# Two 256-column gate tiles in the halves of one PSUM bank instead of in two banks

## The chip, the cores and the metric

The kernel runs on one core of a Trainium2 chip. The metric is the device time of one execution in microseconds (us): the median of the runs, lower is better. A second execution of each kernel is recorded by the hardware profiler; the rows below come from it.

The engines in this text are PE (TensorE, the matrix unit; it writes its results only into PSUM, the accumulator memory of eight banks), ACT (ScalarE), DVE (VectorE), POOL (GpSimd) and SP (which issues the DMA transfers). Each engine works through its own list of instructions in order; a semaphore makes an instruction wait for one on another engine.

## The reference, cut to what matters

One decoder layer on 256 tokens of width 1024, all in float32: a SwiGLU feed-forward block, three parallel token mixers, and a second feed-forward block, with a layer norm after each.

```
h = x @ w_in + b_in
q_a, k_a, v_a, q_b, k_b, v_b, q_m, gates = split(h)
y_a = sliding_window_gqa(q_a, k_a, v_a, attn_sinks) @ w_proj_swa
y_b = moba_attention(q_b, k_b, v_b) @ w_proj_moba
y_m = memory_cross_attention(q_m, mem, ...) @ w_proj_mem
g = sigmoid(gates.reshape(B, S, 3, 1024))
mixed = (g[:, :, 0] * y_a + g[:, :, 1] * y_b + g[:, :, 2] * y_m) @ w_out
x = layer_norm(ALPHA * x + mixed, ln2_g, ln2_b)
```

The change is in the projection that makes `gates`: 3 branches of 1024 columns for 256 tokens.

## The kernel before

Every float32 weight or activation is held as a high part (`whi`, made by an ACT cast) and a low part (`wlo`, made by a DVE subtraction); `split` makes both. `product` computes one float32 product as three matmuls, high x high, high x low and low x high (lines L209, L210 and L211 in the profile). All weights come in one stream of chunks of 128 x 2048 values, which SP loads in order, ACT and DVE split two chunks ahead, and PE uses.

PSUM is one pool of eight banks, `mm` (also called `acc`). Every `mm.tile([P, 512], F32)` takes one bank, whether or not all 512 columns are used, and gives it back when its last reader is done.

The gates are made feature by token: a **tile** here is 128 features x 256 tokens, 8 input blocks x 3 = 24 matmuls of 256 columns. `gate_chunk(c, b, js)` makes the two tiles j = 0 and 1 of one weight chunk; c is one of four groups of 256 features, b one of three branches. The result goes through `tanh` on ACT (with the bias and a factor of a half, which makes a sigmoid up to scale) into `gates`. Groups c = 0 and 1 use `feature_tile` and the left 256 columns of a bank; groups 2 and 3 use another way of multiplying, with all 512 columns, and are not touched.

The six chunks of groups 0 and 1 are placed by hand between the steps of the three attentions, to give PE work while ACT and DVE do the softmax. `scores(nm)` multiplies queries and keys of mixer a, b or m on PE (L637) and has DVE and ACT do the softmax; `turn(nm, i)` transposes two heads' probabilities on PE (L684) and splits them into `p`; `weigh(nm, i)` multiplies `p` by the values on PE (`ps<-p,vab`) and splits the result into `qk_a` or `qk_b`. The code asks for this order:

```
    turn("a", 2)
    gate_chunk(0, 0)
    weigh("a", 2)
    scores("b")
    gate_chunk(0, 1)
    scores("m")
    gate_chunk(0, 2)
    turn("b", 0)
    gate_chunk(1, 0)
    weigh("b", 0)
    turn_b1 = turn("b", 1)
    gate_chunk(1, 1, (0,))
```

In chunks (1, 1) and (1, 2) the two tiles are asked for apart, with a `weigh` and a `turn` between them. The order on each engine (all but SP) is not the code's own: a scheduler that goes by an estimate of readiness, with the code's order as priority, writes it when the program is built, and inserts the semaphore waits. It keeps two engines from using the same bank at a time.

Of the kernel before, what the change touches and what calls it, by code (L numbers as in the profile page):

```python
# [10 lines left out]
F32 = mybir.dt.float32  # L11
F32R = mybir.dt.float32r
BF16 = mybir.dt.bfloat16
AF = mybir.ActivationFunctionType
# [3 lines left out]
P = 128  # L18
S = 256
# [101 lines left out]
def hybrid_layer(ctx: ExitStack, tc: tile.TileContext, a: dict, out: bass.AP):  # L121
    nc = tc.nc
# [9 lines left out]
    mm = acc = ctx.enter_context(tc.tile_pool(name="mm", bufs=8, space=PSUM))  # L132
# [63 lines left out]
    def weights(key, ahead=2):  # L196
        i = index[key]
        load_to(i + 6)
        part_to(i + ahead)
        return part_of.pop(i)  # L200
# [4 lines left out]
    def product(ps, terms, first=True, last=True):  # L205

        n = len(terms)
        for i, ((lh, ll), (rh, rl)) in enumerate(terms):
            nc.tensor.matmul(ps, lh, rh, start=first and i == 0, stop=False)  # L209
            nc.tensor.matmul(ps, lh, rl, start=False, stop=False)  # L210
            nc.tensor.matmul(ps, ll, rh, start=False, stop=last and i == n - 1)  # L211

    def two(t, *s):
        return tuple(x[s] for x in t)
# [6 lines left out]
    def feature_tile(ps, w, col, x, n=KD):  # L221

        product(ps, [(two(w, ALL, slice(k * 256 + col, k * 256 + col + P)), two(x, ALL, k, ALL)) for k in range(n)])

    def feature_tile_2(ps, w, col, x, ks=range(KD), parts_=(0, 1)):

        for part in parts_:
            for k in ks:
                wk = w[part][:, k * 256 + col : k * 256 + col + P]
                if part == 0:  # L230
                    nc.tensor.matmul(ps, wk, x.both[:, k], start=k == 0, stop=False)  # L231
                else:
                    nc.tensor.matmul(ps[:, S:], wk, x[0][:, k], start=False, stop=k == KD - 1)  # L233

    def added(dst, ps):

        b = work.tile([P, 512], F32, name="b", tag="w")[:, :S]
        nc.scalar.copy(b, ps[:, S:])  # L238
        nc.vector.tensor_add(dst, ps[:, :S], b)
# [23 lines left out]
    def tokens_of(name):  # L263

        both = acts.tile([P, KD, 2, S], F32R, name=name, tag="xT")
        return Parts(both)
# [39 lines left out]
    bcol = const.tile([P, NB], F32, name="bcol")  # L306
# [246 lines left out]
    x1T = tokens_of("x1T")  # L553
# [17 lines left out]
    for j in range(2):  # L571
        ps = mm.tile([P, 512], F32, name="ps")
# [4 lines left out]
    for t in range(2):  # L577
        ps = mm.tile([P, 512], F32, name="ps")
# [127 lines left out]

    gates = acts.tile([P, 2, 6, S], F32, name="gates", tag="A1")

    gate_w = {}

    def gate_chunk(c, b, js=(0, 1)):
        if js[0] == 0:
            gate_w[c, b] = weights(("gt", c, b))
        pss = [mm.tile([P, 512], F32, name="ps") for _ in js]
        if c >= 2:
            for part in range(2):
                for j, ps in zip(js, pss):
                    feature_tile_2(ps, gate_w[c, b], j * P, x1T, parts_=(part,))
        for j, ps in zip(js, pss):
            k = 12 + 8 * b + 2 * c + j  # L720
            g = gates[:, c % 2, 2 * b + j, :]
            if c < 2:
                feature_tile(ps[:, :S], gate_w[c, b], j * P, x1T)
                nc.scalar.activation(g, ps[:, :S], AF.Tanh, bias=bcol[:, k : k + 1], scale=0.5)  # L724
            else:
                added(g, ps)
                nc.scalar.activation(g, g, AF.Tanh, bias=bcol[:, k : k + 1], scale=0.5)
# [14 lines left out]
    weigh("a", 1)  # L742
# [9 lines that stand above are left out]
# [115 lines left out]
```

## Time and profile before

| | |
|---|---|
| median of 3 runs | 573.05 us (572.82 to 573.26) |
| the profiled execution's own time | 573.67 us |
| span of its profile, first to last instruction | 571.9 us |
| PE busy | 561.0 us, 98% of the span |
| DVE busy | 451.7 us, 79% |
| ACT busy | 323.6 us, 57% |
| mean granted TensorE clock | 0.996 of full speed |

The span is 1.8 us less than the execution's own time; what lies around it is start and end. Times in a row count from the span's start. A row of the timeline gives the start of an instruction, how long it lasted, engine, line, operation, tile written and tiles read, shape and number; in brackets how long the engine had stood idle before, and for whom. Instructions of an engine overlap: a matmul of 256 columns lasts 0.28 us, but the next starts 0.12 us after it.

### The profile page before, as it was taken

The page shows a single profiled execution, that of the slowest core. Times are in us where ns is not written, and L with a number is a line of the kernel's source. Part 1 is how long each engine was busy: PE and PEld are TensorE (multiplying, and loading weights), DVE is VectorE, ACT ScalarE, POOL GpSimd, SP SyncE. Part 2 cuts the span into 40 slices and gives each one's busy share as a digit, 9 for nine tenths or more (in the row PEclk, how much of TensorE's full clock was granted, in tenths as well). Part 3 has the DMA queues.
Part 4 walks back from the last instruction along what each step waited for, and adds up shares of the span by engine and source line. Part 5 has one row for each costly group of instructions (what it writes and reads, how often), then busy time and mean ns, then how long its engine had stood idle before and what let it go on. Part 6 is the DMA issues. An engine that isn't in the chain of part 4 may idle for free.

```text
span 571.9 us, 8715 instructions
## 1 busy us (share of the span) xinstructions
PE 561.0 (98%) x3378; PEld 498.4 (87%) x3378; DVE 451.7 (79%) x707; ACT 323.6 (57%) x569; POOL 23.6 (4%) x37
## 2 busy tenths in 40 slices
PE   8999999999999999999999999999999999999994
PEld 7888888888888998999999999888898888888883
DVE  4798768788888998699787677997577777889686
ACT  5777555546653652964975655553564645564600
POOL 2000000000000000000002022210000000000001
PEclk9999999999999999999999999999999999999998
DMA  7877856535665276084053655436654645444502
GB/s 266 301 279 290 291 190 252 179 122 197 223 238 221 74 273 242 6 339 172 15 230 127 220 181 189 177 155 253 234 187 175 219 157 211 148 149 170 198 0 73
DMA packets 18025, 108.98 MB, mean 191 GB/s; under 512 B 2112, under 2 KB 2368, under 8 KB 5696
## 3 DMA queue, kind: packets, MB, share of 16 engines
q1 hardware_dynamic: 17984, 108.43, 51.9%
q8 instruction: 26, 0.43, 0.3%
q14 instruction: 15, 0.12, 0.1%
HBM read 107.37 MB, written 1.05 MB: 190 GB/s over the span
## 4 chain that ended last, share of the span: by engine, by line
PE 92%; ACT 3%; DVE 2%; DMA 1%; issue 0%; SPq 0%; POOLq 0%; DVEq 0%
PE ps L231 29%; PE ps L210 15%; PE ps L209 15%; PE ps L233 15%; PE ps L211 15%; ACT whi L136 1%; DMA xT<-in_xT_dram 1%; ACT sc_b L660 1%; PE ps L684 1%; PE ps L277 1%; DVE sc_b L644 1%; DVE m L649 0%; PE ps L637 0%; ACT gates L724 0%; DVE r L519 0%
## 5 line engine op out<-in xcount | busy, mean ns | idle before, releaser
L136 ACT CAST whi<-raw 128x512 fp32r<-128x512 f32 (+3 forms) x242 | 193.8, 845 | 144.3 <-PE ps L231 73.3
L137 DVE TENSOR_TENSOR wlo<-raw,whi 128x512 fp32r<-128x512 f32 (+3 forms) x242 | 230.1, 984 | 54.3 <-ACT whi L136 51.5
L231 PE MATMUL ps<-x0T,whi 128*128 128x512 f32 x352 | 85.8, 392 | 1.6 <-DVE x0T L137 0.8
L231 PEld LDWEIGHTS ps<-x0T,whi 128*128 128x128 f32 x352 | 64.1, 188 | 14.1 <-ACT whi L136 2.1
L231 PE MATMUL ps<-x2T,whi 128*128 128x512 f32 x288 | 68.8, 391 | 0.0
L231 PEld LDWEIGHTS ps<-x2T,whi 128*128 128x128 f32 x288 | 53.0, 188 | 10.3
L209 PE MATMUL ps<-x1T,whi 128*128 128x256 f32 x192 | 55.2, 288 | 0.3 <-ACT sc_m L660 0.3
L211 PE MATMUL ps<-x1T,wlo 128*128 128x256 f32 x192 | 54.4, 283 | 0.0
L210 PE MATMUL ps<-x1T,whi 128*128 128x256 f32 x192 | 54.4, 283 | 0.0
L210 PE MATMUL ps<-wlo,hh 128*128 128x512 f32 (+1 forms) x142 | 54.1, 381 | 0.0
L209 PE MATMUL ps<-whi,hh 128*128 128x512 f32 (+1 forms) x142 | 54.0, 381 | 0.0
L211 PE MATMUL ps<-whi,hl 128*128 128x512 f32 (+1 forms) x142 | 54.0, 380 | 0.0
L233 PEld LDWEIGHTS ps<-x0T,wlo 128*128 128x128 f32 x352 | 46.1, 191 | 2.6 <-DVE wlo L137 0.3
L233 PE MATMUL ps<-x0T,wlo 128*128 128x256 f32 x352 | 46.9, 283 | 0.0
L233 PEld LDWEIGHTS ps<-x2T,wlo 128*128 128x128 f32 x288 | 36.9, 191 | 1.4
L209 PEld LDWEIGHTS ps<-x1T,whi 128*128 128x128 f32 x192 | 36.8, 192 | 0.8 <-ACT sc_m L660 0.5
L233 PE MATMUL ps<-x2T,wlo 128*128 128x256 f32 x288 | 37.4, 283 | 0.0
L210 PEld LDWEIGHTS ps<-x1T,whi 128*128 128x128 f32 x192 | 36.8, 192 | 0.0
L211 PEld LDWEIGHTS ps<-x1T,wlo 128*128 128x128 f32 x192 | 36.8, 192 | 0.0
L238 ACT COPY b<-ps 128x256 f32<-128x256 f32 x92 | 30.7, 368 | 1.0 <-PE ps L233 0.6
L211 PEld LDWEIGHTS ps<-whi,hl 128*128 128x128 f32 x142 | 26.7, 188 | 5.1
L209 PEld LDWEIGHTS ps<-whi,hh 128*128 128x128 f32 x142 | 26.7, 188 | 5.1
(195 smaller groups left out, 888.1 us busy)
## 6 DMA issues: line engine op xcount, KB each, us to landing
raw<-in_w_dram SPq DMA_DIRECT2D x92, 1024.0 KB, 4.8
raw<-in_w_dram SPq DMA_DIRECT2D x16, 256.0 KB, 5.3
ln<-in_ln_dram SPq DMA_DIRECT2D x3, 1024.0 KB, 6.9
xT<-in_xT_dram SPq DMA_DIRECT2D x4, 256.0 KB, 7.1
x_sb<-in_x_dram SPq DMA_DIRECT2D x1, 1024.0 KB, 7.0
mem<-in_memT_dram SPq DMA_DIRECT2D x1, 1024.0 KB, 6.9
out_dram<-r SPq DMA_DIRECT2D x3, 256.0 KB, 2.1
brow<-in_by_column_dram SPq DMA_DIRECT2D x1, 387.0 KB, 7.7
```

Of the source, the lines that this page charges most:

```text
L136: nc.scalar.copy(hi, src)
L137: return nc.vector.tensor_sub(lo, src, hi.bitcast(F32))
L209: nc.tensor.matmul(ps, lh, rh, start=first and i == 0, stop=False)
L210: nc.tensor.matmul(ps, lh, rl, start=False, stop=False)
L211: nc.tensor.matmul(ps, ll, rh, start=False, stop=last and i == n - 1)
L231: nc.tensor.matmul(ps, wk, x.both[:, k], start=k == 0, stop=False)
L233: nc.tensor.matmul(ps[:, S:], wk, x[0][:, k], start=False, stop=k == KD - 1)
L238: nc.scalar.copy(b, ps[:, S:])
L277: nc.tensor.transpose(ps[:, j * P : (j + 1) * P], src[:, k * P : (k + 1) * P], ident)
L644: nc.vector.scalar_tensor_tensor(sc[:, len(raw), :], dist[nm], -SLOPES[h] / SCALE, ps[:, :w], op0=ALU.mult, op1=ALU.add)
L660: nc.scalar.activation(sc[:, e, c0:c1], raw[e][:, c0:c1], AF.Exp, bias=negm[:, e, t : t + 1], scale=SCALE, accum_out=ssum[:, e, t : t + 1])
L684: nc.tensor.transpose(pt[:, s * n + j * P : s * n + (j + 1) * P], sc[:, 2 * i + s, c : c + P], ident)
```

## The change

For groups c = 0 and 1 both tiles of a chunk share one bank: tile 0 takes columns 0 to 255, tile 1 columns 256 to 511. The bank is taken when tile 0 is asked for and kept in `gate_ps`. The number and size of the matmuls, the activations, splits and transfers stay as they are. Lines after L709 move down by five (L724 becomes L729).

```diff
-    gate_w = {}
+    gate_w, gate_ps = {}, {}
 
     def gate_chunk(c, b, js=(0, 1)):
         if js[0] == 0:
             gate_w[c, b] = weights(("gt", c, b))
-        pss = [mm.tile([P, 512], F32, name="ps") for _ in js]
-        if c >= 2:
+        if c < 2:
+
+            if js[0] == 0:
+                gate_ps[c, b] = mm.tile([P, 512], F32, name="ps")
+            pss = [gate_ps[c, b][:, j * S : (j + 1) * S] for j in js]
+        else:
+            pss = [mm.tile([P, 512], F32, name="ps") for _ in js]
             for part in range(2):
...
             if c < 2:
-                feature_tile(ps[:, :S], gate_w[c, b], j * P, x1T)
-                nc.scalar.activation(g, ps[:, :S], AF.Tanh, bias=bcol[:, k : k + 1], scale=0.5)
+                feature_tile(ps, gate_w[c, b], j * P, x1T)
+                nc.scalar.activation(g, ps, AF.Tanh, bias=bcol[:, k : k + 1], scale=0.5)
```

The scheduler puts other work between the two tiles of a chunk. In the listings below a number behind a name tells tiles apart, and the bracket names the engines whose semaphores the instruction waits for.

On PE around chunk (0, 0) of before, where `ps_2669` and `ps_2670` are its two tiles and `ps_2721` is `weigh("a", 2)`:

```order
L211 MATMUL ps_2669<-x1T_1837,wlo_2474 128x256
L209 MATMUL ps_2670<-x1T_1837,whi_2473 128x256
...
L211 MATMUL ps_2670<-x1T_1837,wlo_2474 128x256
L209 MATMUL ps_2721<-p_2646,vab_2008 128x512 [waits Activation_49]
L210 MATMUL ps_2721<-p_2647,vab_2008 128x512 [waits DVE_49]
L211 MATMUL ps_2721<-p_2646,vab_2008 128x512
L209 MATMUL ps_2721<-p_2653,vab_2008 128x2x128 [waits Activation_49]
```

The same place on PE with the change, where `ps_2669` is the bank of both tiles and `ps_2720` is `weigh("a", 2)`:

```order
L211 MATMUL ps_2669<-x1T_1837,wlo_2474 128x256
L209 MATMUL ps_2720<-p_2646,vab_2008 128x512 [waits Activation_49]
L210 MATMUL ps_2720<-p_2647,vab_2008 128x512 [waits DVE_49]
L211 MATMUL ps_2720<-p_2646,vab_2008 128x512
L209 MATMUL ps_2669<-x1T_1837,whi_2473 128x256 [waits Activation_49]
...
L209 MATMUL ps_2720<-p_2653,vab_2008 128x2x128
```

Three of the six matmuls of `weigh("a", 2)` now stand between the tiles, and the first matmul of tile 1 waits for ACT. Around chunk (0, 1) it is the same with five of the 24 matmuls of `scores("m")` between the tiles.

On PE around `turn("b", 0)` of before, where `ps_2945` is tile 1 of chunk (0, 2), `sc_b` the softmax of mixer b, and `ps_3024` tile 0 of chunk (1, 0):

```order
L211 MATMUL ps_2945<-x1T_1837,wlo_2660 128x256
L684 MATMUL ps_2996<-ident_95,sc_b_2732 128x128 [waits DVE_49,Activation_49]
L684 MATMUL ps_2996<-ident_95,sc_b_2732 128x128 [waits DVE_49] x3
L684 MATMUL ps_3005<-ident_95,sc_b_2732 128x128 [waits Activation_49]
L684 MATMUL ps_3005<-ident_95,sc_b_2732 128x128
L209 MATMUL ps_3024<-x1T_1837,whi_2815 128x256 [waits Activation_49]
```

The same place on PE with the change, where `ps_2942` is the bank of both tiles of chunk (0, 2), and `ps_3021` that of chunk (1, 0):

```order
L211 MATMUL ps_2942<-x1T_1837,wlo_2660 128x256
L684 MATMUL ps_2993<-ident_95,sc_b_2731 128x128 [waits DVE_49,PE_49]
L684 MATMUL ps_2993<-ident_95,sc_b_2731 128x128 [waits DVE_49] x3
...
L209 MATMUL ps_3021<-x1T_1837,whi_2814 128x256 [waits Activation_49]
...
L209 MATMUL ps_2942<-x1T_1837,whi_2659 128x256 [waits Activation_49]
...
L209 MATMUL ps_3072<-p_2998,vab_2008 128x512 [waits Activation_49]
...
L684 MATMUL ps_3083<-ident_95,sc_b_2731 128x128
L209 MATMUL ps_3021<-x1T_1837,whi_2814 128x256 [waits Activation_49]
```

The first row of this piece is now the end of tile 0: the transposes of `turn("b", 0)` have moved ahead of tile 1 of chunk (0, 2). Behind them come 22 matmuls of tile 0 of chunk (1, 0), then that tile 1, then the last two matmuls of the other; tile 1 of chunk (1, 0) has moved behind `weigh("b", 0)` and one transpose of `turn("b", 1)`. The order on SP, and so that of all transfers, is unchanged. On ACT and DVE a few weight casts and subtractions trade places with their neighbours from here on; the order of the tanh, exp and `sc_b` instructions is the same up to chunk (1, 0), where the tanh of tile 0 moves next behind that of (0, 2)'s tile 1.

## Rows read from the trace of the kernel before

**Rows 1.** The page: busy us, share of the span and instructions by engine.

```profile
PE 561.0 (98%) x3378; PEld 498.4 (87%) x3378; DVE 451.7 (79%) x707; ACT 323.6 (57%) x569; POOL 23.6 (4%) x37
```

**Rows 2.** Waits of PE from 250 to 305 us: total, times, longest.

```profile
PE ps L209 <- ACT sc_m L660: 0.3, 1, 0.3
```

**Rows 3.** Timeline of PE around chunk (0, 0): tile 1 starts, weigh, scores.

```profile
255.76 0.28 PE L209 MATMUL ps<-x1T,whi 128*128 128x256 f32 x1
...
258.64 0.40 PE L209 MATMUL ps<-p,vab 128*128 128x512 f32 x1
...
259.34 0.28 PE L209 MATMUL ps<-p,vab 128*128 128x256 f32 x1
...
259.78 0.33 PE L637 MATMUL ps<-qk_b 64*128 64x128 f32 x2
```

**Rows 4.** Timeline of DVE at chunk (0, 0): low part of p for weigh.

```profile
255.92 0.67 DVE L137 TENSOR_TENSOR p<-ps,p 128x512 fp32r<-128x512 f32 x1
```

**Rows 5.** Timeline of ACT at chunk (0, 0): weight cast, then tanh of tile 0.

```profile
256.73 0.62 ACT L136 CAST whi<-raw 128x512 fp32r<-128x512 f32 x1
257.38 0.48 ACT L724 ACTIVATE gates<-ps,bcol 128x256 f32<-128x256 f32 x1
```

**Rows 6.** Timelines where one engine stood ready for another: ACT-PE, then PE-ACT.

```profile
6.63 0.40 ACT L136 CAST whi<-raw 128x256 fp32r<-128x256 f32 x1 [1.31 <-DMA raw<-in_w_dram]
7.08 0.74 PE L231 MATMUL ps<-x0T,whi 128*128 128x512 f32 x2 [0.75 <-ACT whi L136]
264.89 0.28 PE L211 MATMUL ps<-x1T,wlo 128*128 128x256 f32 x1
265.21 0.47 ACT L724 ACTIVATE gates<-ps,bcol 128x256 f32<-128x256 f32 x1 [3.25 <-PE ps L211]
```

**Rows 7.** Timeline of PE: scores m, chunk (0, 2), turn, chunk (1, 0), weigh.

```profile
267.98 1.69 PE L637 MATMUL ps<-km,qk_a 64*128 64x256 f32 x24
269.60 0.39 PE L209 MATMUL ps<-x1T,whi 128*128 128x256 f32 x1
275.45 0.82 PE L684 MATMUL ps<-ident,sc_b 128*128 128x128 f32 x6
276.55 0.39 PE L209 MATMUL ps<-x1T,whi 128*128 128x256 f32 x1 [0.29 <-ACT sc_m L660]
282.41 0.40 PE L209 MATMUL ps<-p,vab 128*128 128x512 f32 x1
283.62 0.27 PE L684 MATMUL ps<-ident,sc_b 128*128 128x128 f32 x1
287.14 0.39 PE L209 MATMUL ps<-p,vab 128*128 128x512 f32 x1
288.53 0.38 PE L684 MATMUL ps<-ident,sc_b 128*128 128x128 f32 x2
```

**Rows 8.** Timeline of PE earlier: weigh("a", 1), turn("a", 2), chunk (0, 0).

```profile
251.18 0.40 PE L209 MATMUL ps<-p,vab 128*128 128x512 f32 x1
252.23 0.82 PE L684 MATMUL ps<-ident,sc_a 128*128 128x128 f32 x6
252.80 0.36 PE L209 MATMUL ps<-x1T,whi 128*128 128x256 f32 x1
```

**Rows 9.** Timeline of DVE: the softmax of b, start and scaling; weight subtractions.

```profile
262.45 1.02 DVE L644 SCALAR_TENSOR_TENSOR sc_b<-dist_b,ps 128x384 f32<-128x384 f32 x2
274.49 2.85 DVE L672 TENSOR_SCALAR sc_b<-sc_b,rs 128x128 f32<-128x128 f32 x12
277.25 1.28 DVE L137 TENSOR_TENSOR wlo<-raw,whi 128x512 fp32r<-128x512 f32 x2
```

**Rows 10.** Timeline of ACT: the tanh of (0, 2) after the exps of m.

```profile
279.09 0.85 ACT L724 ACTIVATE gates<-ps,bcol 128x256 f32<-128x256 f32 x2
```

**Rows 11.** The end: last matmul; a stretch, PE to POOL busy, clock, DMA.

```profile
563.67 0.28 PE L211 MATMUL ps<-whi,hl 128*128 128x256 f32 x1
567.00:568.00 1.00, 0.00 (x0) 0.00 (x0) 1.00 (x4) 0.00 (x0) 0.00 (x0) 0.90 0.00 0
```

## Prediction

> **What bounds the kernel now.** I read the page first. PE is busy 561.0 of 571.9 us [rows 1], and no other engine comes near it. Next I read the waits of PE in the stretch that the change touches, 250 to 305 us: one wait of 0.3 us in 55 us [rows 2]. So PE bounds this stretch, its list of instructions is a queue without holes, and whatever holes the change makes in it go into the time one for one: everything later in the kernel stands behind them on PE, and the engines that feed PE (ACT and DVE with the next weight splits, SP with the next loads) only get further ahead. Last I read the timelines of PE, ACT and DVE side by side, to see how long after a gate tile its tanh runs. Chunk (0, 0) is the plainest case: PE begins tile 1 at 255.76, right after tile 0 [rows 3], while the tanh of tile 0 runs at 257.38, because ACT is busy with a weight cast until then [rows 5]. Before, nobody minds: tile 1 has a bank of its own.
>
> **What the change costs, place by place.** The arithmetic is the same, instruction for instruction. New are the waits of tile 1 for the tanh of tile 0, and the moves that the scheduler makes around them. Three prices are needed. From the end of a matmul to the ACT instruction that waits for it: 264.89 + 0.28 = 265.17, start 265.21, so 0.04. From the end of an ACT instruction to the matmul that waits: 6.63 + 0.40 = 7.03, start 7.08, so 0.05 [rows 6]. A tanh lasts 0.47 to 0.48 [rows 5, 6].
>
> The pages bear on the first question, whether the two halves really exclude each other. Rows of before show no case of one engine reading half of a bank while PE writes the other. The Trainium skill (PSUM — Partial Sum Buffer, section "PSUM bank collisions raise a hardware error") says they must not: two engines on one bank collide even at different addresses, so a kernel has to guard by bank. By that rule the waits in the change's order are needed and cost what follows; guarded by address, they and the moves would be gone and the sum would be zero.
>
> (A) Chunk (0, 0). Tile 0 is done at 255.76 as before. The first weigh matmul takes 0.23 ((259.34 - 258.64) / 3, [rows 3]), to 255.99. The second needs the low part of `p`, which DVE finishes at 255.92 + 0.67 = 256.59 [rows 4]; plus 0.05 it starts at 256.64: a hole of 0.65. Two of 0.23 bring PE to 257.10. Tile 1 needs the tanh, which ends at 257.38 + 0.48 = 257.86 [rows 5], plus 0.05: 257.91, a hole of 0.81. Up to here ACT and DVE do what they did before, so these times stand. Together **1.46**.
>
> (B) Chunk (0, 1). ACT is idle when tile 0 ends (it had waited 3.25 us for it, [rows 6]), so the wait is the bare one: from the start of the last matmul 0.28 + 0.04 + 0.47 + 0.05 = 0.84, of which 0.12 is the normal step. That leaves 0.72, and five of 24 matmuls of `scores("m")`, which take 269.60 - 267.98 = 1.62 [rows 7], cover 0.34 of it. **0.38**.
>
> (C) `turn("b", 0)`. Before, its six transposes follow tile 1 of (0, 2) at 275.45, when the scaled softmax of b, whose scaling DVE begins at 274.49 [rows 9], is just there. Now one tile of 2.92 ((275.45 - 269.60) / 2, [rows 7]) has moved behind them, so PE comes early. PE ends tile 0 of (0, 2) at 269.60 + 1.46 + 0.38 + 2.92 = 274.36. The softmax is late itself. Its first DVE step at 262.45 [rows 9] stands behind the split of `weigh("a", 2)`, which on ACT now stands behind a weight cast and the tanh of tile 1. Those weights are overwritten once tile 1 is almost done, at 257.91 + 22 x 0.12 + 0.28 = 260.83; cast at 260.87, tanh 0.52 later, first `qk_a` cast 0.37 later at 261.76, to 262.13; two more weight casts have to pass on ACT, at 262.02 and 262.54, so the second `qk_a` cast comes at 263.06; on DVE two subtractions of about 0.6 [rows 9] pass between the two, to 263.79, then the second `qk_a` step of 0.34: the softmax starts at 264.13, or 1.7 later than before. (Steps of 0.52, 0.37 and 0.34 are my estimates: the rows' 0.62, 0.48 and their like less the 0.10 by which neighbours on an engine overlap, as in 0.85 for two tanh [rows 10].) The least shift is A's 1.46, the most I take as 2.0. So scaling begins at 274.49 + 1.7 = 276.19. Twelve instructions take 2.85 [rows 9], 0.24 each; the fourth ends at about 277.19, the fourth transpose starts 0.05 later, and three steps of 0.10 (0.57 / 6, [rows 8]) bring PE to 277.54. PE spends 277.54 - 274.36 = 3.18 here where before it spent 276.55 - 275.45 = 1.10 [rows 7]. **2.08**, with 1.85 to 2.4 for the shift's bounds.
>
> (D) Tile 1 of (0, 2). Its tanh stands on ACT behind the eight exps of mixer m, at 279.09 [rows 10], and these behind the exps of b; with the same shift 280.79, to 281.27, and PE starts at 281.32. The 22 matmuls in front, 22 x 0.122 = 2.68, bring PE from 277.54 to 280.22 only. **1.10**. The shift cancels here, since both ends carry it.
>
> (E) Tile 1 of (1, 0). The tile of (D) and two matmuls end at 284.48, `weigh("b", 0)` takes 1.05, one transpose 0.10: 285.63. On ACT a weight cast that waits for (D)'s tile (at 284.32), the tanh of that tile and then the needed one (285.21 to 285.69) allow 285.74. **0.11**; if the order on ACT slips by a cast, up to 0.6.
>
> (F) Small stalls that disappear. Before, `weigh("b", 0)` and `weigh("b", 1)` take 283.62 - 282.41 = 1.21 and 288.53 - 287.14 = 1.39 [rows 7], where one that waits for nothing takes 252.23 - 251.18 = 1.05 [rows 8]. PE now comes to both about 3 us later than the splits they wait for. **-0.50**. That `turn("b", 0)` before took 1.10 and not 0.57 [rows 8] is already in C.
>
> (G) Chunks (1, 1) and (1, 2): nothing. A weigh and a turn, 1.05 + 0.57 = 1.62 us of PE work [rows 8], already lie between their tiles, more than twice the bare 0.72; without that cover each would cost up to 0.72. Loads and splits: nothing, as they wait for PE (weight buffers) or run ahead of it.
>
> The sum is 1.46 + 0.38 + 2.08 + 1.10 + 0.11 - 0.50 = **4.6 us**. The profiled execution took 573.67, so it would take 578.3; that execution lies 0.6 above the median of the timed runs, which would go from 573.05 to 577.7. Each of the six waits may cost 0.1 more than the bare 0.05 (at 276.55 the chain of several waits looks slower), and PE has some start-up to repeat after a hole; I forecast **577.8**. The forecast's own range is 576.9 to 578.9: C's bounds, up to 0.5 from E, up to 0.5 from the waits.
>
> **The rivals.** *Cover works (cheaper).* The scheduler put work between the tiles in order to cover the waits. If the splits of `weigh("a", 2)` come earlier relative to PE than in this trace, A falls to what the bare wait leaves after three weigh matmuls, 0.72 - 0.70, about nothing, and D loses its 1.10 if ACT runs that tanh before the exps of m. Against it: the order on ACT is fixed, and the rows of A are measured. 573.05 + 4.6 - 1.46 - 1.10 = 575.1; with A alone covered 576.2.
>
> *Freed bank (not slower).* Chunks now hold one bank instead of two, and one of the few stalls of PE before, the 0.29 at 276.55, is a wait for a bank that ACT still reads. If the halves cost no wait, all stalls of this stretch could go: 0.53 in the turn and 0.50 in the two weighs, so 572.0. It decides when the softmax of b is scaled by the time that PE comes to the transposes. Against it: with no hole at all in front, PE would be there at 269.60 + 2.92 = 272.52, and the scaling began at 274.49 when nothing was late [rows 7, 9].
>
> *Clock.* The hole in C is 2.2 us, longer than any in the rows. At the kernel's end the granted clock is full until about 567.8 (0.90 as a mean of 1 and a half over 567 to 568), 3.9 us after the last matmul at 563.67 ended, and then half, 1.2 GHz [rows 11]. So an idle PE does lose the clock, and here two holes and a turn drawn out over 3.2 us follow each other. Were (1, 0) and the next tile to run at the half level, 5.6 us of matmuls would take 11.2: 583.4. Against it: 2.2 us after that last matmul the clock was still full. The Trainium skill (TensorE: Matmul & The Clock Gate, Part 1) says that the gate halves the clock when PE has been idle, which the last row bears out.
>
> *Later harm.* Holes move PE against the weight stream; if a split or load that was just in time becomes late, 1 to 2 us more, 579.5. The waits of before show no such place.
>
> **How the numbers follow.** The forecast has 0.80, cover 0.09, later harm 0.05, clock 0.03, freed bank 0.03. The range for 8 in 10 is the forecast's own, widened to take in A covered and a part of later harm: 576.2 to 579.4. What a measurement of this kernel can tell from no change is about 0.2%, 1.1 us. Slower by more: all of forecast, harm and clock and most of cover, 0.95; within 0.2%: 0.03; faster: 0.02.
>
> **What the profile of the changed kernel would show.** PE's waits between 250 and 305 us sum to some 5 us instead of 0.3, and name ACT `gates` at three places (about 257, 267, 281 us) and DVE `sc_b` once, the longest, about 2 us (A and C also name DVE `p`). Tile 1 of (0, 0) starts near 257.9, the transposes of `sc_b` near 276.5, `weigh("b", 2)` some 4.6 us later than before. After 305 us every stage takes as long as before. A granted clock below 1 between 270 and 300 us, a missing wait on `sc_b`, or an offset that shrinks later would make the prediction wrong.

## The result

The changed kernel takes **578.49 us** (median of 5 runs, 578.21 to 578.92) where the kernel before takes 573.10 (5 runs, 572.82 to 573.43). The ratio is 1.0095, with a 95% interval of 1.0084 to 1.0106: slower by 5.4 us. The forecast was 577.8, its range 576.2 to 579.4.

### The profile page after: what moved, and what is told of

Same layout as the page of the kernel before. It is cut to its first block, busy times and chain, and to the rows that moved or that the text cites. A ratio compares the mean times of both kernels' runs of the same rounds, so it can differ in the third digit from the quotient of the medians.

```text
span 576.7 us, 8716 instructions
## 1 busy us (share of the span) xinstructions
PE 563.3 (98%) x3378; PEld 499.6 (87%) x3378; DVE 452.3 (78%) x707; ACT 324.1 (56%) x569; POOL 23.6 (4%) x37
## 3 DMA queue, kind: packets, MB, share of 16 engines
HBM read 107.37 MB, written 1.05 MB: 188 GB/s over the span
## 4 chain that ended last, share of the span: by engine, by line
PE 51%; DVE 2%; ACT 1%; issue 1%; POOLq 0%; DVEq 0%
PE ps L231 15%; PE ps L209 9%; PE ps L210 9%; PE ps L211 9%; PE ps L233 8%; ACT sc_b L660 1%; PE ps L684 1%; DVE sc_b L644 1%; DVE m L649 0%; DVE wlo L137 0%; ACT whi L136 0%; PE ps L277 0%; DVE r L519 0%; POOLq L868 0%; PE ps L831 0%
```

## The profile after

The page of the changed kernel, busy time by engine and the granted clock in 40 slices of the span of 576.7 us (compare [rows 1]):

```profile
PE 563.3 (98%) x3378; PEld 499.6 (87%) x3378; DVE 452.3 (78%) x707; ACT 324.1 (56%) x569; POOL 23.6 (4%) x37
...
PEclk9999999999999999999899999999999999999999
```

PE has the same 3378 matmuls but is busy 2.3 us longer, and one slice of the clock is an 8. The other 2.5 us of the longer span are idle time. The waits of PE from 250 to 305 us, total, times and longest, where before had one line of 0.3 us [rows 2]:

```profile
PE ps L684 <- DVE sc_b L672: 2.2, 1, 2.2
PE ps L209 <- ACT gates L729: 0.6, 1, 0.6
PE ps L210 <- DVE p L137: 0.5, 1, 0.5
```

The longest is the one that the prediction named, for `sc_b`. ACT `gates` stands there once and not three times, and the waits sum to 3.3 us and not to some 5. The timeline of PE shows the places (start, length; in brackets the idle time before and for whom):

```profile
256.00 0.50 PE L210 MATMUL ps<-p,vab 128*128 128x512 f32 x1 [0.51 <-DVE p L137]
...
257.30 0.39 PE L209 MATMUL ps<-x1T,whi 128*128 128x256 f32 x1 [0.59 <-ACT gates L729]
...
266.67 0.38 PE L209 MATMUL ps<-x1T,whi 128*128 128x256 f32 x1
266.89 0.28 PE L210 MATMUL ps<-x1T,whi 128*128 128x256 f32 x1
...
276.45 1.53 PE L684 MATMUL ps<-ident,sc_b 128*128 128x128 f32 x6 [2.21 <-DVE sc_b L672]
277.63 0.56 PE L209 MATMUL ps<-x1T,whi 128*128 128x256 f32 x1
...
280.33 0.28 PE L209 MATMUL ps<-x1T,whi 128*128 128x256 f32 x1
...
281.39 0.40 PE L209 MATMUL ps<-x1T,whi 128*128 128x256 f32 x2
```

Two holes at chunk (0, 0), a split of the scores of m at 266.67, the large hole ahead of the transposes, and then chunk (1, 0) from 277.63. Its first 12 matmuls, to 280.33, take 2.70 us, where before they took 1.54 (276.55 to 278.09). The windows of that stretch (length, busy time and instructions of PE, PEld, DVE, ACT and POOL, granted clock, DMA share, GB/s) say why:

```profile
274.00:276.00 2.00, 0.24 (x3) 0.04 (x1) 0.24 (x2) 2.00 (x10) 0.00 (x0) 1.00 0.00 0
276.00:277.00 1.00, 0.55 (x3) 0.42 (x3) 0.99 (x6) 1.00 (x3) 0.00 (x0) 0.94 0.00 0
277.00:278.00 1.00, 1.00 (x6) 0.92 (x6) 1.00 (x6) 1.00 (x6) 0.00 (x0) 0.50 0.02 8
...
279.00:280.00 1.00, 1.00 (x7) 1.00 (x6) 1.00 (x2) 1.00 (x5) 0.00 (x0) 0.50 0.00 0
280.00:281.00 1.00, 1.00 (x9) 1.00 (x9) 0.26 (x2) 1.00 (x6) 0.00 (x0) 0.85 0.00 0
281.00:282.00 1.00, 1.00 (x11) 1.00 (x10) 0.98 (x4) 1.00 (x4) 0.00 (x0) 1.00 0.00 0
```

The clock was still full while PE stood, fell to half (1.2 GHz) just as PE had started again, and was full again in 281 to 282. Of the two matmuls merged at 281.39 the second, at 281.51, is the first of tile 1 of chunk (0, 2). It came without a wait that the trace shows. The tanh of tile 0 that it needs runs on ACT behind the last exp of m, as forecast:

```profile
280.17 0.48 ACT L660 ACTIVATE sc_m<-ps,negm 128x256 f32<-128x256 f32 x1
...
280.62 0.49 ACT L729 ACTIVATE gates<-ps,bcol 128x256 f32<-128x256 f32 x1
```

It ends at 281.11, 0.4 us ahead of that matmul. Whether the clock or the tanh is the loss of this place is the first question for the experiments. The second is what sets the price of chunk (0, 0).

To compare the kernels, the table has the length of three stretches of PE's list, from the first matmul of one chunk to that of another, worked out from the starts in each trace's timeline; what an execution loses ahead of chunk (0, 0) does not enter. "Landing" is when ACT starts the weight cast that waits for a transfer, counted from the start of chunk (0, 0). "Over before" is the difference of the medians in the same job.

| kernel | over before, us | (0, 0) to (0, 1) | (0, 1) to (0, 2) | (0, 2) to (1, 1) | landing |
|---|---|---|---|---|---|
| before | | 9.24 | 7.55 | 14.59 | 0.48 |
| the changed kernel | 5.39 | 11.07 | 8.13 | 18.24 | 0.77 |
| only (0, 0) shared | 2.53 | 10.72 | 7.56 | 15.20 | 0.43 |
| only (0, 1) shared | -0.07 | 9.24 | 8.13 | 14.03 | 0.88 |
| only (0, 2) shared | 2.92 | 9.24 | 7.55 | 18.10 | 1.23 |
| only (1, 0) shared | 4.22 | 9.24 | 7.55 | 19.28 | 0.72 |
| only (1, 1), (1, 2) shared | 0.22 | 9.24 | 7.55 | 14.60 | 1.43 |
| none shared, order of the change | 2.77 | 9.24 | 7.55 | 18.00 | 1.75 |
| changed, fillers in the hole | 5.38 | 11.05 | 8.13 | 18.00 | 0.74 |
| changed, two banks for (0, 2) | 5.22 | 13.66 | 8.13 | 18.07 | 1.86 |
| changed, both | 4.63 | 10.54 | 8.13 | 17.33 | -0.42 |
| only (0, 0), weight split later | 0.77 | 9.36 | 7.55 | 15.18 | |
| changed, weight split later | 3.82 | 9.36 | 8.13 | 18.24 | |

Behind (1, 1) these kernels are as fast as before, but for 0.34 that belongs to term F: from there to the first matmul of chunk (2, 0) it is 25.1 us in before and with (0, 0) alone, 24.8 in the changed kernel and with (0, 2) or (1, 0) alone.

## The experiments

In the diffs `mms` and `turned_mm` hold the matmuls of the gate tiles and the transposes, `tanh` the activations, `highs` and `lows` the casts and subtractions of a weight chunk; `queue_behind(x, others)` places the others behind x on their engine. Added lines shift the line numbers in some rows by two to five.

### One chunk at a time

Each of these kernels shares the bank for some chunks only; the diff shows the first, against the changed kernel, and the others differ in the condition.

```diff
-        if c < 2:
+        if (c, b) == (0, 0):
...
             pss = [gate_ps[c, b][:, j * S : (j + 1) * S] for j in js]
+        elif c < 2:
+            pss = [mm.tile([P, 512], F32, name="ps")[:, :S] for _ in js]
         else:
```

Only (0, 0):

> Only chunk (0, 0) shares a bank; the other five chunks keep two banks and the order of before. The trace of the changed kernel puts PE 1.84 us late behind this chunk (holes of 0.78 and 0.74 and slow first steps behind each). If the sum of places holds, the whole kernel is 1.8 us slower (1.5 to 2.0), because the softmax of b shifts by about as much and so the small stalls of before stay behind it. If the loss of (0, 0) were taken up by the stalls that stand behind it in the kernel before (0.53 in the turn, 0.46 for the exps of m, 0.50 in two weighs), it would be 0.3 to 0.9 only. If it starts the clock loss as well, 3 or more.

575.51 against 572.98, ratio 1.0051 (1.0036 to 1.0066). That is 2.5 slower, more than the 1.5 to 2.0 expected. The six runs go from 574.61 to 577.47, wider than any other kernel so far. In the profiled one (575.17) the chunk costs 1.48, and the stretch behind (0, 2) another 0.61, so nothing of it is taken up later. What the upper runs lose has to come from something that varies; more on it below.

Only (0, 1):

> Only chunk (0, 1) shares a bank. In the changed kernel its hole costs about 0.5 us. Here ACT and DVE are not late, so the stalls of before in the turn of b (0.53) and at the exps of m (0.46) wait for times that do not move. If holes add up place by place: 0.4 to 0.5 us slower. If a hole ahead of a later wait for ACT or DVE is taken up by that wait: 0.0 (-0.2 to 0.2).

572.91 against 572.98, ratio 1.0001 (0.9992 to 1.0009). The chunk itself costs 0.58 (8.13 for 7.55), and the stretch behind it gives 0.56 back (14.03 for 14.59): PE's delay eats into the stalls at the turn and at the exps of m. The second theory holds: a hole ahead of a later wait is free.

Only (0, 2):

> Only chunk (0, 2) shares a bank: the transposes of b move ahead of its tile 1. With nothing late in front, PE ends tile 0 near 272.5 (times of before) and the turn ends near 275.8, 3.3 us instead of 1.10, so 2.2 for the move; 1.1 for the tanh behind the exps of m, or the clock in its place; less 0.5 for stalls that go. My sum says 2.8 us slower (2.3 to 3.2). If clock and tanh wait add up: 3.9 or more. If the move alone costs and the wait is covered: 1.7.

575.90, ratio 1.0048 (1.0036 to 1.0060): 2.9 slower, where the sum said 2.8. Clock and tanh do not add up.

Only (1, 1) and (1, 2):

> Only chunks (1, 1) and (1, 2) share a bank, whose tiles the code already asks for with a weigh and a turn between them. If 1.6 us of PE work covers a wait of 0.72 us, the time is that of before: 0.0 (-0.2 to 0.2), and the order on PE is unchanged. If every shared pair costs its bare wait: 1.4 us slower. If two banks fewer help the turns: faster by up to 0.5.

573.20 against 572.98, ratio 1.0007 (0.9999 to 1.0015): no change that can be told, every stretch as before. (One of the twelve runs took 575.25.) The cover of term G holds.

Only (1, 0):

> Only chunk (1, 0) shares a bank. In the changed kernel its hole is 0.14 us, since tile 1 stands behind the whole weigh and 3 us of holes lie in front. Here the scheduler moves five of the six matmuls of the weigh of b ahead of tile 1, and PE has lost nothing in front of them, so they wait for the casts of p on ACT and DVE. If prices belong to chunks: 0.1 us slower (0 to 0.3). If they hang on what was lost in front: 2 to 3 us slower, with a hole of 1.2 to 1.6 at the first matmul of the weigh and one at the second.

577.39 against 573.17, ratio 1.0070 (1.0057 to 1.0084): 4.2 slower, the dearest single chunk and more than the 2 to 3 expected, though in the changed kernel its hole is 0.14. The waits of PE from 279 to 284 us, and where they stand behind the transposes of b:

```profile
PE ps L210 <- DVE p L137: 1.4, 1, 1.4
PE ps L209 <- ACT p L136: 0.8, 1, 0.8
```

```profile
275.08 0.82 PE L684 MATMUL ps<-ident,sc_b 128*128 128x128 f32 x6
...
280.10 0.49 PE L209 MATMUL ps<-p,vab 128*128 128x512 f32 x1 [0.78 <-ACT p L136]
...
281.98 0.50 PE L210 MATMUL ps<-p,vab 128*128 128x512 f32 x1 [1.38 <-DVE p L137]
```

And the windows behind them:

```profile
283.00:284.00 1.00, 0.95 (x6) 0.75 (x7) 1.00 (x3) 0.80 (x2) 0.00 (x0) 0.93 0.00 0
284.00:285.00 1.00, 1.00 (x6) 1.00 (x6) 1.00 (x3) 0.00 (x0) 0.00 (x0) 0.50 0.55 82
...
286.00:287.00 1.00, 1.00 (x7) 1.00 (x7) 0.00 (x0) 0.00 (x0) 0.00 (x0) 0.50 0.98 418
```

Five matmuls of the weigh stand ahead of tile 1 here and wait for `p`, and then the clock falls, which I had not put into the expectation. That the price hangs on what was lost in front, as the second theory has it, is not shown by this: the order differs as well. Here one gate tile stands between the transposes of b and the weigh, which begins 5.02 us after the first of them (280.10 - 275.08), 0.78 of it waiting. Its second matmul, which needs the low part of `p`, could go after 6.90 (281.98 - 275.08). In the changed kernel two tiles stand there, one of them tile 1 of (0, 2), and the weigh begins 8.18 us after the first transpose (284.63 - 276.45); before there are two as well, and it begins after 6.96 (282.41 - 275.45, [rows 7]). Neither trace shows a wait for `p`. So one tile less in front of the weigh, a matter of order, is the likelier reason; no run separates the two.

### Order without sharing

No chunk shares a bank; the code asks for the order that the scheduler made in the changed kernel.

```diff
-    gate_chunk(0, 2)
+    gate_chunk(0, 2, (0,))
     turn("b", 0)
-    gate_chunk(1, 0)
+    gate_chunk(1, 0, (0,))
+    gate_chunk(0, 2, (1,))
     weigh("b", 0)
+    gate_chunk(1, 0, (1,))
```

> No chunk shares a bank; only the order of the changed kernel around chunk (0, 2) is written into the code: the transposes of b ahead of its tile 1, tile 1 of (1, 0) behind the weigh. If the move is what costs there, 2.5 us slower than before (2.0 to 3.2) without any shared bank, and about the same as with (0, 2) alone shared. If the shared bank costs by itself, 0 to 0.5.

575.76 against 572.99, ratio 1.0041 (1.0029 to 1.0053): 2.8 slower, with not one bank shared, about as much as the 2.9 with (0, 2) alone shared. PE waits once from 250 to 305 us, and then the clock falls:

```profile
PE ps L684 <- DVE sc_b L672: 2.5, 1, 2.5
```

```profile
275.00:276.00 1.00, 1.00 (x7) 0.92 (x6) 1.00 (x6) 1.00 (x5) 0.00 (x0) 0.50 0.03 8
276.00:277.00 1.00, 1.00 (x7) 1.00 (x7) 1.00 (x6) 1.00 (x7) 0.00 (x0) 0.50 0.00 0
```

So what costs at (0, 2) is the place of the transposes, not the bank: they stand a tile too early, the clock falls behind the hole, and the wait for the tanh adds nothing to the two.

### Clock or tanh at tile 1 of (0, 2)

Two edits of the changed kernel, alone and together, each with PE's order of the changed kernel held at (0, 2) (tile 1 behind the 22nd matmul of (1, 0)). The first fills the hole with matmuls on zeros:

```diff
     gate_chunk(0, 2)
+    fill = mm.tile([P, 512], F32, name="ps")
+    filler = [nc.tensor.matmul(fill[:, :P], idle, idle, start=True, stop=True) for _ in range(32)]
+    queue_behind(mms[0, 2, 0][-1], filler)
     turn("b", 0)
+    for f in filler:
+        queue_behind(f, turned_mm["b", 0])
     gate_chunk(1, 0)
```

The second gives (0, 2) its two banks back (`if c < 2 and (c, b) != (0, 2):`), in the order of the code of the experiment before. There tile 1 of (1, 0) stands ahead of all transposes of `turn("b", 1)` and not behind the first, which by itself makes the way from the weigh to (1, 1) 4.51 us (287.15 to 291.66) instead of 4.72 (284.63 to 289.35 in the changed kernel).

> The changed kernel with its order on every engine, and 32 small matmuls on zeros (their result is not read) between tile 0 of chunk (0, 2) and the transposes of b, which fill most of the 2.2 us hole. The granted clock should then stay full. If clock and tanh wait cover one another (22 matmuls at full clock take 2.7 us and then PE waits 1.1 us for the tanh), the time is that of the changed kernel: 0.0 (-0.3 to 0.2). If the fall of the clock is the loss of this place, 1.0 to 1.3 us faster than the changed kernel, so 4.2 slower than before instead of 5.4. If the clock falls in spite of the fillers, nothing changes and the trace shows 0.5 again.

> The changed kernel with the same order on PE, but chunk (0, 2) has two banks again, so that its tile 1 waits for no tanh; the hole at the transposes and the fall of the clock stay. If either of the two suffices to set the time here, the same as the changed kernel: -0.1 (-0.4 to 0.2). If the tanh wait is the loss of this place: 1.1 us faster than the changed kernel.

> Both at once: fillers in the hole, and two banks for chunk (0, 2), in the order of the changed kernel. If each of the two hides the other, only this kernel gains: 1.0 to 1.3 us faster than the changed one, while each alone gains nothing. If one of them is the whole loss, this one is as fast as the one that removes it. A new wait for the split of p in the weigh of b (up to 0.7) could take a part back.

Fillers: 578.37 against 572.99, ratio 1.0089 (1.0076 to 1.0102). Two banks: 578.21, ratio 1.0100 (1.0083 to 1.0118). Both: 577.62, ratio 1.0077 (1.0064 to 1.0090). By the medians each alone leaves the 5.4 of the changed kernel standing, and both together take 0.8 off (4.63 for 5.38 with fillers alone), but the intervals of the three overlap, and what (0, 0) costs varies. The stretch from (0, 2) to (1, 1) leaves out what varies ahead of it: 18.24, then 18.00, 18.07 and 17.33. Less the 0.2 of the other order, two banks alone gain nothing, fillers alone 0.24 and both 0.7. The fillers on PE, their clock, and the waits of the kernel with fillers, with the first matmul of tile 1 of (0, 2):

```profile
274.18 1.96 PE L758 MATMUL ps<-idle 128*128 128x128 bf16 x32
```

```profile
277.00:278.00 1.00, 0.73 (x5) 0.37 (x4) 1.00 (x6) 1.00 (x5) 0.00 (x0) 1.00 0.02 8
278.00:279.00 1.00, 0.82 (x6) 0.82 (x7) 1.00 (x6) 1.00 (x7) 0.00 (x0) 1.00 0.00 0
```

```profile
PE ps L209 <- ACT gates L731: 0.8, 2, 0.6
...
PE ps L209 <- ACT sc_m L662: 0.5, 1, 0.5
PE ps L686 <- DVE sc_b L674: 0.4, 1, 0.4
```

```profile
281.26 0.39 PE L209 MATMUL ps<-x1T,whi 128*128 128x256 f32 x1 [0.18 <-ACT gates L731]
```

With a full clock the wait for the tanh comes back (ACT `gates` twice instead of once), if only with 0.18 us, and so does the wait for a bank that the exps of m still read, since the fillers take one more bank. That wait, 0.45 us, stands ahead of the other and covers most of it, and it is part of why both edits together gained 0.7 and not the 1.0 to 1.3 expected. In kind the gap is as expected: each of the two causes hides the other. How much is due to each is not cleanly shown, since the fillers brought a third.

### What sets the price of (0, 0)

In the kernel with two banks for (0, 2) two of six runs took 580.7 (the profiled one 580.79) and the rest 577.7 to 578.2. Its trace shows the difference at chunk (0, 0), which had not been touched: 13.66 us to (0, 1). ACT first:

```profile
253.66 0.62 ACT L136 CAST whi<-raw 128x512 fp32r<-128x512 f32 x1 [3.80 <-DMA raw<-in_w_dram]
```

Then PE behind it, and the clock behind that:

```profile
255.96 0.49 PE L209 MATMUL ps<-p,vab 128*128 128x512 f32 x1 [1.05 <-ACT p L136]
256.98 0.50 PE L210 MATMUL ps<-p,vab 128*128 128x512 f32 x1 [0.52 <-DVE p L137]
...
258.29 0.38 PE L209 MATMUL ps<-x1T,whi 128*128 128x256 f32 x1 [0.58 <-ACT gates L733]
```

```profile
258.00:259.00 1.00, 0.71 (x6) 0.71 (x7) 1.00 (x3) 0.23 (x1) 0.00 (x0) 0.99 0.00 0
259.00:260.00 1.00, 1.00 (x7) 1.00 (x6) 0.21 (x1) 0.00 (x0) 0.00 (x0) 0.50 0.00 0
```

Chunk (0, 0) started at 251.80, so the transfer was seen 1.86 us after it. In before ACT took up that cast 0.48 us after the start at 252.80:

```profile
253.28 0.62 ACT L136 CAST whi<-raw 128x512 fp32r<-128x512 f32 x1 [2.48 <-DMA raw<-in_w_dram]
```

ACT stands on a cast of weights for (1, 0), which are needed some 25 us later, and behind that cast on ACT stand the casts of `p` that the weigh needs and the tanh that tile 1 needs. The column "landing" of the table goes with the price of the chunk: 1.30 at -0.42, 1.48 at 0.43, 1.81 at 0.74, 1.83 at 0.77, and 4.42 at 1.86, where the half clock adds its part. Where (0, 0) has two banks, landings from 0.48 to 1.75 cost nothing. That a late landing is also behind the longest of the timed runs is argued, not shown: only one execution of each kernel has a trace, and with two banks everywhere one of 21 runs of before took 575.73, which nothing here explains. To test what the cast's place does, that split is queued behind the tanh and the split of `p`, with (0, 0) alone shared, and in the whole changed kernel:

```diff
-    turn("a", 2)
+    turn_a2 = turn("a", 2)
     gate_chunk(0, 0)
...
     gate_chunk(0, 1)
+    queue_behind(turn_a2, lows[index["gt", 1, 0]])
+    queue_behind(tanh[0, 0, 0], highs[index["gt", 1, 0]])
     scores("m")
```

> Only chunk (0, 0) shares a bank, and the split of the weights of (1, 0), whose transfer ACT waits for (2.3 to 3.8 us in the traces so far) ahead of the casts of p and the tanh, is queued behind them on ACT and DVE. If the place of that weight cast on ACT is what makes (0, 0) dear, most of its loss goes: 0.3 to 0.9 us slower than before instead of 2.5, and the runs lie closer together than the 574.6 to 577.5 of the kernel with (0, 0) alone shared, since the landing of the transfer no longer counts. If the loss is that of a bare wait for a tanh that is as early as it can be: still 1.5 or more.

> The changed kernel, all six chunks shared, with the same reorder on ACT and DVE: the split of the weights of (1, 0) behind the casts of p and the tanh of (0, 0). If terms add up place by place, it gains what chunk (0, 0) gains: 1.2 to 1.8 us faster than the changed kernel, 3.6 to 4.2 slower than before. If the hole at the transposes takes up what is won in front, since the softmax of b stays late: 0.0 to 0.3.

With (0, 0) alone: 573.94 against 573.17, ratio 1.0010 (1.0001 to 1.0018), 0.8 slower where it was 2.5, and eleven runs within 573.54 to 574.19. The chunk costs 0.12 (9.36 for 9.24). PE goes from the weigh to tile 1 without a hole:

```profile
255.21 0.40 PE L212 MATMUL ps<-p,vab 128*128 128x512 f32 x1
255.45 0.40 PE L213 MATMUL ps<-p,vab 128*128 128x512 f32 x1
255.68 0.39 PE L214 MATMUL ps<-p,vab 128*128 128x512 f32 x1
255.94 0.39 PE L212 MATMUL ps<-x1T,whi 128*128 128x256 f32 x1
```

What is left, 0.6, is in the stretch from (0, 2) (15.18): the scaling of the softmax of b starts at 274.65, 22.39 after the chunk's start at 252.26, where it was 21.69 (274.49 less 252.80, [rows 8, 9]). The whole changed kernel: 576.99, ratio 1.0067 (1.0054 to 1.0079), 1.6 us less than the changed kernel (3.82 for 5.39 over before). The first theory holds in both: the price of (0, 0) was the place of a weight split, whose cast on ACT waits for a transfer.

### A kernel without the small stalls

Two banks, and from chunk (1, 0) on each weigh one gate tile later:

```diff
-    turn("b", 0)
-    gate_chunk(1, 0)
+    gate_chunk(1, 0, (0,))
+    turn("b", 0)
+    gate_chunk(1, 0, (1,))
+    gate_chunk(1, 1, (0,))
     weigh("b", 0)
     turn_b1 = turn("b", 1)
-    gate_chunk(1, 1, (0,))
+    gate_chunk(1, 1, (1,))
     weigh("b", 1)
     turn("b", 2)
-    gate_chunk(1, 1, (1,))
+    gate_chunk(1, 2, (0,))
     weigh("b", 2)
     turn("m", 0)
-    gate_chunk(1, 2, (0,))
+    gate_chunk(1, 2, (1,))
     weigh("m", 0)
     turn("m", 1)
-    gate_chunk(1, 2, (1,))
     weigh("m", 1)
```

> Two banks everywhere, as before; tile 0 of chunk (1, 0) is asked for ahead of the transposes of b, and from there each weigh stands one gate tile later, so that the softmax of b, the exps of m and the splits of p have one tile (2.9 us) more. If the small stalls of before (0.53 in the turn, 0.46 at the exps of m, 0.50 in two weighs) are pure lateness, 0.5 to 1.0 us faster than before. If they move on to the last weigh of m, which now has no tile in front of it: 0.0. If ACT and DVE cannot use the room because casts of p stand behind weight casts: up to 1.5 slower.

572.91 against 573.17, ratio 0.9994 (0.9985 to 1.0003): not to be told from before. PE's waits from 250 to 305 us are this one, at the last weigh of m, which has lost its cover:

```profile
PE ps L209 <- ACT p L136: 0.5, 1, 0.5
```

The stalls of before are gone, and this one stands at the end. From (0, 0) to chunk (2, 0) the profile has 56.19 us (252.51 to 308.70), where before has 56.50 (252.80 to 309.30), so most of the stalls' 1.0 us (0.53 in the turn and 0.50 in the weighs) is lost again there. No version here beats the kernel before by more than a measurement can tell.

## Where the prediction held and where it did not, step by step

The sign and the places were right, and the time lay 0.7 above the forecast, within the range. The mechanism was right for the moved transposes and the holes at (0, 0), but not whole. The prediction named a granted clock below 1 between 270 and 300 us as a sign of being wrong, and the clock was at half from 276.9 to 280.3 (0.94 over 276 to 277, 0.85 over 280 to 281). Not all of the loss is idle time of PE, as the sum had it: for 2.3 of the 4.8 us by which the span grew PE counts as busy, with the same matmuls. In the traces chunk (1, 1) and what follows lie later, counted from the start of (0, 0), by 5.7 us in the end, where the sum said 4.6; the profiled execution of the changed kernel began (0, 0) at 251.91, 0.89 before that of the other, which takes it to the 4.8 by which the two spans differ. That 4.8 lies so near 4.6, and that the absolute times in the forecast of the profile came out (276.45 for 276.5), is luck: no term had that earlier start.

- **(A), 1.46: measured 1.83 in the profiled execution.** The step that failed is "Up to here ACT and DVE do what they did before, so these times stand". They hang on a transfer whose landing moves against PE from one execution to the next. Here it landed 0.29 later after the start of (0, 0) than in before (0.77 for 0.48), which makes most of the 0.37 missing; at a landing of 0.43 the price was 1.48, as summed. The price was 1.30 to 4.42 in five traces, and 0.12 with one split out of the way. The argument against the first rival, that the order on ACT is fixed, was right; that the rows fix the size was not.
- **(B), 0.38: measured 0.58, and worth nothing by itself.** The 0.20 more is slow steps where PE goes from one product to another without any wait: at 266.67 the next matmul comes 0.22 later instead of 0.12, and there are two more such changes than before. But PE then waits for the softmax anyway, so (B) only makes the hole of (C) shorter, which the sum took into account, as it counts (C) from behind (B); alone it costs -0.07.
- **(C), 2.08: measured 2.45** (from the end of tile 0 of (0, 2), at 273.96 + 0.12 = 274.08, to (1, 0) at 277.63 are 3.55 us, where the sum had 3.18, less the same 1.10 of before [rows 7]). The move of the transposes is the cost, with or without a shared bank. Mis-sized was the shift of the softmax, put at 1.7 with 2.0 as the most: its scaling began at 276.02, 24.11 after the start of (0, 0) instead of 21.69, so 2.42. Of the 0.72 missing, 0.37 is (A)'s. The rest arises on ACT and DVE: that the softmax shifts by more than PE I had put at 0.24 (1.7 less 1.46), and it is 0.59 (2.42 less 1.83), and 0.58 in the kernel with (0, 0) alone and the weight split later, where PE loses only 0.12. From the start of the scaling to (1, 0) it took 1.61 instead of 1.35.
- **(D), 1.10: measured 1.14, but not by the cause that I gave** (22 matmuls in 281.51 - 277.63 = 3.88, where before they take 2.74, 276.55 to 279.29). The step that failed is the path: what set the start of tile 1 was the fall of the clock, which the sum had at nothing and which takes 2.70 - 1.54 = 1.16 here. The wait for the tanh, which the sum had, would at full clock have held tile 1 until 281.11 + 0.05 = 281.16, or 0.79 (an estimate from these rows). That the two are of one size, so that the number came out, is luck.
- **(E), 0.11, and (F), -0.50: 0.14 and -0.50.** With the slow steps around it (E) is 0.22. The second weigh of b takes 1.05 (292.30 to 293.35), where it took 1.39 [rows 7].
- **(G), nothing: right.**

Of the rivals, the clock came true as an event and not as a cost. It fell, but for 12 matmuls and not for 5.6 us of them, over a stretch most of which had to wait for the tanh in any case. The reason that I gave against it, a clock still full 2.2 us after the last matmul of the kernel, did not carry over: the hole was 2.21 us long and the clock fell at 276.9, with PE at work again. The freed bank is not shown: the wait for the exps of m [rows 2] is gone in the changed kernel, but also with no bank shared in the order of the change, and it stays with (0, 0) or with (1, 1) and (1, 2) alone shared (0.4 and 0.3). The rival of covered work is what the weight split in another place makes of (A). No harm came later.

The rule by which two engines may not use two halves of one bank at once was not put to the test: no kernel here leaves these waits out. What the bank itself costs, apart from the scheduler's order, is shown only where the order is the same: with (0, 2) in the order of the change the tanh wait is worth about 0.5 (18.00 against 17.33 with fillers, less the 0.2 of the other order at (1, 0)), and nothing beside a fallen clock.

## What to carry to other kernels

A wait put between two tiles costs what stands in front of its releaser on the releasing engine, and what the scheduler moves to fill it: look at both before the wait itself, and write a moved step down as a change of its own. Holes don't add up: one ahead of a later wait is free, and two causes that end at the same place hide one another, so that taking either away gains little or nothing. Where a chain goes back to a transfer, the gap in one trace is a sample; look for a cast that waits for a transfer and is needed much later than what stands behind it.

## What the runs showed of the hardware that was not expected

- The granted clock was 1.00 while PE stood for 2.2 us and 0.50 once it worked again (277 to 280 us). It also fell in a stretch whose longest wait of PE was 1.05 us, with 0.52 and 0.58 behind it, and did not fall behind 0.51 and 0.59 alone (256 to 258 us of the changed kernel). With 32 matmuls on zeros in the large hole, 1.96 us of work, it stayed at 1.00. The Trainium skill (TensorE: Matmul & The Clock Gate, Part 1) says that the gate follows how busy PE was lately; these rows agree with that.
- At 1.2 GHz the 256-column matmuls of this kernel start 0.21 us apart instead of 0.12 (ten steps from 277.99 to 280.13), so a fall costs 0.09 a matmul.
- The same transfer was seen by ACT between 0.88 us before (in the kernel without the small stalls) and 1.86 us after the same matmul, in kernels whose work on PE up to there is the same.
